# A second 2x2 scheme inside a pair of feed-forward blocks: product 4 joins product 2

## The chip, the cores and the metric

The kernel runs on one core of a Trainium2 chip. The metric is the device time of one execution in microseconds, the median of several runs; smaller is better. TensorE (PE) multiplies, with weights loaded by its own load path (PEld); VectorE (DVE), ScalarE (ACT) and GpSimd (POOL) do the element-wise work; SyncE (SP) issues nearly all transfers.

## What is computed

One layer of a decoder trunk on 1056 tokens (1024 of a prompt and 32 of samples), all in float32. The change lies in the first half of its two feed-forward networks:

```
h = LN1(alpha*x + 0.5*SwiGLU_a(x))
z = h @ w_in + b_in                     # attention and a gated MLP on z
h = LN2(alpha*h + mix @ w_out)
y = LN3(alpha*h + 0.5*SwiGLU_b(h))
def swiglu(x, w1, w3, w2):              # w1, w3: 1024 x 2816, w2: 2816 x 1024
    return (jax.nn.silu(x @ w1) * (x @ w3)) @ w2
```

## The kernel before

**Precision.** A float32 number is split in a rounded high part and the rest: ACT casts the high part (line 254), DVE subtracts it from the number (line 255). Each 128x128x264 product then takes three matmuls (`mm3`, line 243): high by high, high by low, low by high.

**Seven products for eight.** A block f is 128 columns of w1 together with the same 128 of w3. Its work is a 2x2 matrix product: the rows are w3 and w1, the inner halves are the two halves of the 1024 inputs, the columns are two neighbouring pieces of 264 tokens. There are two such column pairs, `x` = 0 and 1. The Strassen-Winograd scheme does it in seven products, numbered 1 to 7 and used in the order 1, 2, 6, 7, 5, 4, 3 or near it. One product is KH = 4 slices of 128 inputs x 2 column pairs x 3 matmuls = 24 matmuls (`product`). The combined weights are made for each block by `parts13`: two loads of 512 KB (`ab` is w3, `cd` is w1), four sums on POOL (lines 445, 446, 450, 451; on DVE for the first blocks), and six splits into tiles W. The combined inputs (`self.T`) are made once for a stage by `spread`.

**A pair of blocks.** Product 2 uses the second input half of w3 alone. For two successive blocks f and g it is again a 2x2 product: the rows are the blocks, the inner halves are halves of those 512 inputs, the columns are x = 0 and 1. `hidden_pair` therefore does the two product 2 together in seven inner products of 2 x 3 = 6 matmuls, 42 rather than 48; their weights come from `parts_two` (one load, four sums of 256 columns on POOL, three splits), their inputs from `spread_two`, once a stage. So a pair has 6 x 2 outer products of 24 and 42 inner matmuls, 330. `half` is the generator that runs one block's outer products. There are ten pairs in each of the two networks; in the first, one block is left over and runs before them in `hidden`.

**Around it.** After a pair `spill_sums` makes seven combinations of the hidden values for the w2 stage, four of them by a subtraction on DVE (line 701), splits them and stores them (lines 697, 698). It runs in the background queue `bg`; each call of `step` takes three pieces from that queue and moves the next block's `parts13` on by one piece. `ready(f)` finishes the weights of f and starts those of the block after it. `advance(two)` moves `parts_two` on.

**Buffers.** Tiles named W are weights (8 buffers); R are raw loads and Q the sums on POOL (2 each); M (6) and S (37) are working tiles. PSUM has 3 banks `mm` and 5 `ax`; outer products use mostly ax, inner ones mm.

**Order.** A list scheduler (`schedule_with_timeline_sim=True`) places each engine's instructions by its own estimate of readiness; work inside `urgent()` goes ahead of other ready work. Each engine then runs its list strictly in order.

Of the kernel before, what the change touches and what calls it, by code (L numbers as in the profile page):

```python
# [21 lines left out]
P = 128  # L22
# [62 lines left out]
class Trunk:  # L85
# [339 lines left out]
    def parts13(self, src, f, engine):  # L425
# [22 lines left out]
        part(4, cd[:, hi])  # L448
# [12 lines left out]
    def parts_two(self, w13, f):  # L461

        nc, H, q = self.nc, KH * P, KH * P // 2
        with self.tc.high_priority(offset=URGENT):
            raw = self.R([P, D]).rearrange("p (f x) -> p f x", f=2)
            dma = nc.sync.dma_start(raw, w13[f : f + 2, 1, :, H:].rearrange("f p x -> p f x"))
# [11 lines left out]
        one, four = self.S([P, 2, H], F32R), self.M([P, 2, q], F32R)  # L478
# [3 lines left out]
        h, l = self.S([P, 4, q], F32R), self.S([P, 4, q], F32R)  # L482
        self.split(h, l, s)
        self.L2 = {1: (one[:, 0, :q], one[:, 1, :q]), 2: (one[:, 0, q:], one[:, 1, q:]), 4: (four[:, 0], four[:, 1])}
        for i, p in enumerate((5, 6, 7, 3)):
            self.L2[p] = (h[:, i], l[:, i])
        yield

    def spread_two(self, y0, y1):

        nc = self.nc
        b11, b21, b12, b22 = y0[:, :2], y0[:, 2:], y1[:, :2], y1[:, 2:]
        one, two = self.T[0][2], self.T[1][2]
        rows = lambda hi, lo: [(hi[:, k], lo[:, k]) for k in range(2)]
        pick = lambda t, o: [x[:, o : o + 2] for x in t]
        T = self.T2 = {1: rows(*pick(one, 0)), 2: rows(*pick(one, 2)), 3: rows(*pick(two, 2))}

        def sub(a, b):
            t = self.M([P, 2, C])
            nc.vector.tensor_tensor(t, a, b, op=ALU.subtract)  # L500
            return t

# [7 lines left out]
        t1 = sub(b12, b11)  # L510
        yield
        t2 = sub(b22, t1)
        put(5, t1, pick(two, 0))
        yield
        t3 = sub(b22, b12)
        put(6, t2)
        yield
        t4 = sub(b21, t2)
# [66 lines left out]
    def half(self, f):  # L585
# [16 lines left out]
        go(three, 7, lambda x: copy(h[:, x, 1], three[x]), True)  # L602
        yield h
        go(one, 6, lambda x: copy(h[:, x, 0], one[x]))
        yield
        go(three, 4, lambda x: tt(h[:, x, 0], three[x], h[:, x, 0], op=ALU.add))
        yield
        go(one, 5, lambda x: tt(h[:, x, 1], one[x], h[:, x, 1], op=ALU.add))  # L608
        with self.urgent():
            for x in range(2):  # L610
                nc.scalar.activation(h[:, x], h[:, x], AF.Silu)  # L611
# [4 lines left out]
    def hidden_pair(self, f, g, w13, ready, step):  # L616

        nc = self.nc
        copy = nc.scalar.copy
        two = self.parts_two(w13, f)  # L620
        a, b = self.half(f), self.half(g)
# [1509 lines left out]
```

## Time and profile before

| what | value |
|---|---|
| median of 3 runs | 2142.72 us (2141.47 to 2144.37) |
| the profiled execution's own time | 2141.25 us |
| its span, first to last instruction | 2139.3 us, mean clock 0.994 |
| busy: PE, DVE, ACT, POOL | 98%, 74%, 44%, 17% of the span |
| DMA | 436.99 MB, mean 204 GB/s |

The pairs of the first network run from about 66 to 455 us, those of the second from about 1400 to 1860 us; the w2 stages follow them. In the rows of the profile, a group reads: line, engine, operation, output<-input by the program's names, shapes, count | busy us, mean ns of one | idle time of the engine just before, and what ended most of it. In a list by order of time the first two numbers are the start and the duration in us.

### The profile page before, as it was taken

What the parts mean: (1) busy time and instruction counts of PE and PEld (TensorE: products, weight loads), DVE (VectorE), ACT (ScalarE), POOL (GpSimd) and SP (SyncE); (2) the same over time, 40 slices, a digit from 0 to 9 for tenths busy, and PEclk for the clock granted to TensorE, in tenths of its full rate; (3) what the DMA queues carried; (4) which work ended last, traced back from release to release, by engine and by line L of the source; (5) the groups of instructions that cost most, each with busy time, mean ns of one, the idle gap of its engine ahead of it and who ended that gap; (6) DMA issues with size and microseconds to landing.
All of it is one profiled execution on the core that took longest, in us unless ns stands there. A gap on an engine that the chain in (4) does not pass through costs nothing.

```text
span 2139.3 us, 43300 instructions
## 1 busy us (share of the span) xinstructions
PE 2103.2 (98%) x17163; PEld 2069.3 (97%) x17163; DVE 1587.7 (74%) x2915; ACT 941.0 (44%) x1897; POOL 363.8 (17%) x329
## 2 busy tenths in 40 slices
PE   9999999999999999999999989999999999999997
PEld 8999999998999999999988889999999999999997
DVE  8877777767789846988767558787777777757886
ACT  5544444422124643445476543164545545522224
POOL 0234334300000022332000000000433433300000
PEclk9999999999999999999999999999999999999998
DMA  4365565599884346676756655432446545597852
GB/s 155 117 206 175 184 222 175 180 367 354 306 332 176 123 144 213 221 250 216 276 190 198 195 166 173 151 118 98 168 172 213 194 138 183 202 355 294 307 180 82
DMA packets 172954, 436.99 MB, mean 204 GB/s; under 512 B 24576, under 2 KB 58992, under 8 KB 170064
## 3 DMA queue, kind: packets, MB, share of 16 engines
q1 hardware_dynamic: 172320, 433.70, 58.0%
q8 instruction: 134, 2.20, 0.4%
q14 instruction: 68, 0.56, 0.1%
q10 hardware_dynamic: 432, 0.54, 0.1%
HBM read 314.80 MB, written 165.57 MB: 225 GB/s over the span
## 4 chain that ended last, share of the span: by engine, by line
PE 87%; DMA 7%; DVE 4%; SPq 1%; issue 1%; ACT 1%; ACTq 0%; DVEq 0%
PE ax L243 48%; PE mm L243 35%; DMA S<-sumsA 1%; DMA R<-w2pb 1%; DMA R<-w2pa 1%; DMA S<-sumsB 1%; DMA S<-hD 1%; PE ax L1428 1%; PE ax L1477 1%; DMA S<-cD 1%; PE ax L1454 1%; DVE W L255 0%; DVE S L843 0%; DVE S L255 0%; DMA cD<-S 0%
## 5 line engine op out<-in xcount | busy, mean ns | idle before, releaser
L243 PE MATMUL ax<-S,W 128*128 128x264 f32 x7392 | 989.5, 285 | 5.2 <-ACT W L254 4.9
L243 PEld LDWEIGHTS ax<-S,W 128*128 128x128 f32 x7392 | 936.9, 188 | 7.2 <-ACT W L254 5.4
L243 PE MATMUL mm<-S,W 128*128 128x264 f32 x5232 | 735.4, 287 | 14.2 <-DVE S L1807 4.8
L243 PEld LDWEIGHTS mm<-S,W 128*128 128x128 f32 x5232 | 674.7, 189 | 25.4 <-DVE S L1807 6.7
L243 PE MATMUL mm<-S,S 128*128 128x264 f32 x1944 | 284.5, 286 | 0.8 <-DVE S L1147 0.6
L243 PEld LDWEIGHTS mm<-S,S 128*128 128x128 f32 x1944 | 255.2, 188 | 2.6 <-issue 0.6
L254 ACT CAST W<-R 128x512 fp32r<-128x512 f32 (+4 forms) x214 | 137.6, 658 | 245.3 <-PE mm L243 66.2
L255 DVE TENSOR_TENSOR W<-R,W 128x512 fp32r<-128x512 f32 (+4 forms) x214 | 175.5, 824 | 67.2 <-ACT W L254 65.7
L243 PE MATMUL ax<-S,S 128*128 128x264 f32 x1488 | 218.0, 284 | 0.0
L243 PEld LDWEIGHTS ax<-S,S 128*128 128x128 f32 x1488 | 196.4, 188 | 0.2 <-issue 0.2
L255 DVE TENSOR_TENSOR W<-Q,W 128x512 fp32r<-128x512 f32 (+2 forms) x199 | 148.2, 761 | 57.5 <-ACT W L254 57.2
L254 ACT CAST W<-Q 128x512 fp32r<-128x512 f32 (+2 forms) x199 | 128.6, 678 | 81.9 <-DVE Q L392 78.4
L1042 DVE SCALAR_TENSOR_TENSOR S<-ax,S 128x264 f32<-128x264 f32 x240 | 99.4, 429 | 51.7 <-PE ax L243 51.0
L111 POOL CAST S<-ones 128x1 fp32r<-128x1 f32 x36 | 12.8, 363 | 625.7 <-PE ax L243 381.5
L611 ACT ACTIVATE S<-S 128x528 f32<-128x528 f32 x80 | 47.2, 638 | 140.9 <-DVE S L608 140.9
L255 DVE TENSOR_TENSOR S<-Q,S 128x1024 fp32r<-128x1024 f32 (+1 forms) x59 | 65.6, 1113 | 25.2 <-ACT S L254 25.2
L445 POOL TENSOR_TENSOR Q<-R 128x512 f32<-128x512 f32 x36 | 48.1, 1335 | 204.0 <-DVE W L255 74.5
L1256 ACT ACTIVATE S<-ax,cols 128x264 f32<-128x264 f32 (+5 forms) x99 | 40.4, 496 | 87.5 <-PE ax L243 83.1
L473 POOL TENSOR_TENSOR Q<-R 128x256 f32<-128x256 f32 x20 | 20.9, 1045 | 341.0 <-DVE W L255 270.3
L254 ACT CAST S<-Q 128x1024 fp32r<-128x1024 f32 (+1 forms) x59 | 56.9, 965 | 34.6 <-DVE Q L403 32.1
L651 DVE TENSOR_TENSOR M<-M,M 128x264 f32<-128x264 f32 x60 | 63.4, 1083 | 11.2 <-ACT M L657 11.2
L599 ACT COPY M<-ax 128x264 f32<-128x264 f32 x80 | 26.9, 376 | 95.1 <-issue 88.1
(246 smaller groups left out, 2305.8 us busy)
## 6 DMA issues: line engine op xcount, KB each, us to landing
ws<-st SPq DMA_DIRECT2D x144, 256.0 KB
S<-sumsA SPq DMA_DIRECT2D x63, 528.0 KB
S<-sumsB SPq DMA_DIRECT2D x63, 528.0 KB
R<-w13b SPq DMA_DIRECT2D x54, 512.0 KB
R<-w13a SPq DMA_DIRECT2D x52, 512.0 KB
M<-kv SPq DMA_DIRECT2D x96, 256.0 KB
sumsA<-M SPq DMA_DIRECT2D x90, 264.0 KB
sumsB<-M SPq DMA_DIRECT2D x90, 264.0 KB
```

The costliest lines, as they stand in the source:

```text
L243: mm = lambda a, b, s, e: nc.tensor.matmul(o, a[:, cc], b, start=s, stop=e, skip_group_check=True)
L254: a = self.nc.scalar.copy(hi, src)
L255: b = self.nc.vector.tensor_tensor(lo, src, hi.bitcast(F32), op=ALU.subtract)
L445: tt(s12[:, lo], cd[:, lo], cd[:, hi], op=ALU.add)
L599: go(one, 1, lambda x: copy(r[:, x], one[x]), True)
L611: nc.scalar.activation(h[:, x], h[:, x], AF.Silu)
L651: nc.vector.tensor_tensor(t, t, m, op=ALU.add)
L1042: nc.vector.scalar_tensor_tensor(y(x, r, e), bank[x], HALF, y(x, r, e), op0=ALU.mult, op1=ALU.add)
L1256: nc.scalar.activation(o, view(bank[x]), fn, bias=b, scale=sc)
L1428: m = nc.tensor.matmul(pS[h][:, r, :nk], q[e, i * P : (i + 1) * P], k[e, k0 : k0 + nk], start=True, stop=True)
L1454: nc.tensor.transpose(pT[r][:, h, o], s[:, r, h, o], self.ident)
L1477: nc.tensor.matmul(pv[0][e, (i % 4) * P : (i % 4 + 1) * P], V[:, i - (nb - 1) + b, e], sT[:, r, h, b * P : b * P + P], start=b == 0, stop= ...
```

## The change

Product 4 uses the second input half of w1 alone, so the two products 4 of a pair form a 2x2 product in the same way. The change treats them as product 2 was treated: `parts_two` takes a `row` (1 for w3, 0 for w1) and is called twice for a pair, `spread_two` takes the product's number n and is called for 2 (on DVE, as before) and for 4 (its eight sums and differences on POOL: the inputs are first put together again from their parts). `parts13` no longer makes the part for product 4, so it has five splits. A pair is 5 x 2 outer products and 2 x 42 inner matmuls, 324.

It also rearranges the pair: the seven inner products for w3 now run among the outer products of the first block, those for w1 among the second's. Most inner results are added by DVE straight from PSUM to the accumulators; before, ACT copied more of them out and DVE added the copies. `parts_two` of the next pair's w3 (`ahead`) is made during this pair. The weights of the inner products move from S to W tiles. `ready(g)` is called one product earlier. In `spill_sums`, three of the four subtractions go from DVE to POOL.

```diff
     def parts13(self, src, f, engine):
...
-        part(4, cd[:, hi])
...
-    def parts_two(self, w13, f):
+    def parts_two(self, w13, f, row):
...
-            dma = nc.sync.dma_start(raw, w13[f : f + 2, 1, :, H:].rearrange("f p x -> p f x"))
+            dma = nc.sync.dma_start(raw, w13[f : f + 2, row, :, H:].rearrange("f p x -> p f x"))
...
-        one, four = self.S([P, 2, H], F32R), self.M([P, 2, q], F32R)
+        one, four = self.W([P, 2, H]), self.M([P, 2, q], F32R)
...
-        h, l = self.S([P, 4, q], F32R), self.S([P, 4, q], F32R)
+        h, l = self.W([P, 4, q]), self.W([P, 4, q])
...
-    def spread_two(self, y0, y1):
+    def spread_two(self, n, engine, *raw):
...
+        def value(j, o):
+            if raw:
+                return raw[j][:, o : o + 2]
+            return make(*(x.bitcast(F32) for x in pick(self.T[j][n], o)), ALU.add)
...
     def half(self, f, r=None):
...
-        one, r = (ax(), ax()), self.M([P, 2, C])
-        go(one, 1, lambda x: copy(r[:, x], one[x]), True)
+        one = ax(), ax()
+        if r is None:
+            r = self.M([P, 2, C])
+            go(one, 1, lambda x: copy(r[:, x], one[x]), True)
+        else:
+            go(one, 1, lambda x: tt(r[:, x], r[:, x], one[x], op=ALU.add), True)
...
-        go(one, 6, lambda x: copy(h[:, x, 0], one[x]))
-        yield
-        go(three, 4, lambda x: tt(h[:, x, 0], three[x], h[:, x, 0], op=ALU.add))
+        go(one, 6, lambda x: tt(h[:, x, 0], one[x], h[:, x, 1], op=ALU.add))
...
+    def inner(self, row, p, bank, act, first=False):
+        n = 2 if row else 4
+        while p not in self.T2.get(n, ()):
+            self.step(self.bg, 1)
+        for k in range(2):
+            self.mm3(bank, self.L2[row].pop(p) if k else self.L2[row][p], k * P, *self.T2[n][p][k], first and k == 0, k == 1)
+        with self.urgent():
+            act(bank)
+
+    def hidden_pair(self, f, g, ready, step, two, ahead):
...
+        r = next(a)
+        step(f)
+        x, y = bank(), bank()
+        do(1, 1, x, add(r[:, 0]), True)
+        do(1, 2, y, add(r[:, 0]), True)
+        h = next(a)
+        step(f)
+        self.advance(two)
+        do(1, 6, x, copy(s[:, 0]))
+        y = bank()
+        do(1, 7, y, copy(s[:, 1]), True)
+        next(a)
...
+        do(1, 5, x, add(s[:, 1]))
+        do(1, 4, y, add(s[:, 0]))
+        next(a)
...
+        next(b)
...
+        ready(g)
+        do(1, 3, x, add(r[:, 1]))
+        next(a)
...
+        i = next(b)
+        step(g)
+        self.advance(ahead)
+        x, y = bank(), bank()
+        do(0, 1, x, add(h[:, 0, 0]), True)
+        do(0, 2, y, add(h[:, 0, 0]), True)
...
     def spill_sums(self, i, a, b):
...
-        sub = lambda t, u, v: nc.vector.tensor_tensor(t, u, v, op=ALU.subtract)
+        sub = lambda t, u, v, e=nc.gpsimd: e.tensor_tensor(t, u, v, op=ALU.subtract)
...
     def ffn(self, w13, w2p, w2, i, mode, resid):
...
+        twos = [lambda y=(self.Y[0][1], self.Y[2][1]): self.spread_two(2, nc.vector, *y)]
+        twos.append(lambda: self.spread_two(4, nc.gpsimd))
...
+            for _ in ahead:
+                pass
+            ready(f)
+            ahead = two(queue[0], 1) if queue else None
+            self.hidden_pair(f, g, ready, step, two(f, 0), ahead)
```

What the scheduler makes of it at the passage from one pair to the next. Line numbers are each kernel's own. POOL before, the four sums of one block's weights (into Q) and the four of `parts_two`:

```order
L445 TENSOR_TENSOR Q_2231<-R_2194 128x512
L446 TENSOR_TENSOR Q_2231<-Q_2231,R_2193 128x512
L450 TENSOR_TENSOR Q_2280<-R_2193,R_2194 128x512
L451 TENSOR_TENSOR Q_2280<-R_2193,Q_2231 128x512
L473 TENSOR_TENSOR Q_2370<-R_2289 128x256
L475 TENSOR_TENSOR Q_2370<-R_2289 128x256
```

POOL now, the same place (445, 446, 449 and 450 are the weights' sums, 719 the spill's subtractions):

```order
L445 TENSOR_TENSOR Q_2296<-R_2258 128x512
L719 TENSOR_TENSOR S_1818<-S_2062,S_1818 128x2x264
L719 TENSOR_TENSOR M_2300<-S_2062,M_2299 128x528
L449 TENSOR_TENSOR Q_2359<-R_2257,R_2258 128x512
L446 TENSOR_TENSOR Q_2296<-Q_2296,R_2257 128x512
L719 TENSOR_TENSOR M_2362<-S_2062,M_2300 128x528
L450 TENSOR_TENSOR Q_2359<-R_2257,Q_2296 128x512
```

Three subtractions stand between the four sums, and each is behind a sum that needs a loaded R tile. DVE before, from the last products of a pair (line 678) on; 701 are the spill's subtractions, 255 the splits:

```order
L678 TENSOR_TENSOR S_1743<-S_1743,M_1694 128x2x264
L255 TENSOR_TENSOR W_2147<-Q_2032,W_2147 128x512
L613 TENSOR_TENSOR S_2002<-S_2002,ax_1910 128x264
L613 TENSOR_TENSOR S_2002<-S_2002,ax_1911 128x264
L701 TENSOR_TENSOR M_2234<-S_1743 128x528
L701 TENSOR_TENSOR M_2235<-S_2002,M_2234 128x528
L701 TENSOR_TENSOR S_1743<-S_2002,S_1743 128x2x264
L255 TENSOR_TENSOR W_2228<-R_2193,W_2228 128x512
L255 TENSOR_TENSOR S_1743<-S_1743,M_2237 128x2x264
L255 TENSOR_TENSOR M_2234<-M_2234,M_2243 128x528
```

DVE now, there (638 are inner results added from a bank mm, 615 an outer one from ax):

```order
L696 TENSOR_TENSOR S_1818<-S_1818,M_1752 128x2x264
L719 TENSOR_TENSOR M_2299<-S_1818 128x528
L255 TENSOR_TENSOR W_2254<-Q_2188,W_2253 128x1024
L638 TENSOR_TENSOR M_2266<-M_2266,mm_2314 128x264
L255 TENSOR_TENSOR W_2293<-R_2257,W_2293 128x512
L255 TENSOR_TENSOR S_1818<-S_1818,M_2304 128x2x264
L638 TENSOR_TENSOR M_2266<-M_2266,mm_2315 128x264
L615 TENSOR_TENSOR S_2332<-ax_2264,S_2332 128x264
L255 TENSOR_TENSOR M_2299<-M_2299,M_2309 128x528
L615 TENSOR_TENSOR S_2332<-ax_2265,S_2332 128x264
L255 TENSOR_TENSOR S_1818<-S_1818,M_2364 128x2x264
```

The evictions of mm and ax now stand between splits with both inputs in SBUF; before, only the splits and subtractions stood here.

More of the change, by code (lines that the diff above doesn't have):

```diff
@@ L609, in half @@
         with self.urgent():
-            for x in range(2):
-                nc.scalar.activation(h[:, x], h[:, x], AF.Silu)
+            nc.scalar.activation(h[:, :, 1], h[:, :, 1], AF.Silu)
         yield
@@ L623, in hidden_pair @@
+    def hidden_pair(self, f, g, ready, step, two, ahead):
+        nc = self.nc
+        bank = lambda: self.mm_tile()[:, :C]
+        copy = lambda t: lambda b: nc.scalar.copy(t, b)
+        add = lambda t: lambda b: nc.vector.tensor_tensor(t, t, b, op=ALU.add)
+        do = self.inner
+        s = self.M([P, 2, C])
+        a, b = self.half(f), self.half(g, s)
+        r = next(a)
         step(f)
-        h.append(next(a))
+        x, y = bank(), bank()
+        do(1, 1, x, add(r[:, 0]), True)
+        do(1, 2, y, add(r[:, 0]), True)
+        h = next(a)
@@ L636, in hidden_pair @@
         ready(g)
+        do(1, 3, x, add(r[:, 1]))
+        next(a)
+        step(g)
+        self.advance(two)
         del self.L[f]
-        while len(self.T2) < 7:
-            self.step(self.bg, 1)
-        def inner(p, bank, act, first=False):
-            hi, lo = self.L2[p]
-            for k in range(2):
-                self.mm3(bank, (hi, lo), k * P, *self.T2[p][k], first and k == 0, k == 1)
-            with self.urgent():
-                act()
-        def add(t, *more):
-            def act():
-                for m in more:
-                    nc.vector.tensor_tensor(t, t, m, op=ALU.add)
-            return act
@@ L655, in hidden_pair @@
-        one, two = self.mm_tile()[:, :C], self.mm_tile()[:, :C]
-        tu, v = self.M([P, 2, C]), self.M([P, C])
-        inner(1, one, lambda: copy(tu[:, 0], one), True)
-        inner(2, two, add(r[0][:, 0], tu[:, 0], two), True)
-        step(g)
-        h.append(next(b))
-        step(g)
-        inner(6, one, lambda: copy(tu[:, 1], one))
-        three = self.ax_tile()[:, :C]
-        inner(7, three, lambda: copy(v, three), True)
+        i = next(b)
+        step(g)
+        self.advance(ahead)
@@ L665, in hidden_pair @@
+        x, y = bank(), bank()
+        do(0, 1, x, add(h[:, 0, 0]), True)
+        do(0, 2, y, add(h[:, 0, 0]), True)
         next(b)
         step(g)
-        inner(5, one, add(r[1][:, 1], v, one))
+        self.advance(ahead)
+        do(0, 6, x, add(i[:, 0, 0]))
+        y = bank()
+        do(0, 7, y, add(i[:, 1, 0]), True)
         next(b)
         step(g)
-        next(b)
-        step(g)
-        inner(4, three, add(r[1][:, 0], tu[:, 1], three))
-        inner(3, one, add(r[0][:, 1], one))
@@ L674, in hidden_pair @@
-        step(g)
-        next(b)
-        with self.urgent():
-            for x, y in zip(h, r):
-                nc.vector.tensor_tensor(x[:, :, 0], x[:, :, 0], y, op=ALU.mult)
-        self.L2 = None
-        step(g)
+        self.advance(ahead)
+        do(0, 5, x, add(i[:, 1, 0]))
+        do(0, 4, y, add(i[:, 0, 0]))
+        step(g)
+        self.advance(ahead)
+        next(b)
+        do(0, 3, x, add(h[:, 1, 0]))
+        with self.urgent():
+            for t, u in ((i, s), (h, r)):
+                nc.scalar.activation(t[:, :, 0], t[:, :, 0], AF.Silu)
+                nc.vector.tensor_tensor(t[:, :, 0], t[:, :, 0], u, op=ALU.mult)
```

84 lines of the change are left out of this document (42 added, 42 removed).

## The prediction

> **What bounds the kernel now.** I read the page's totals first, then the waits of the matmul engine, then the stage that the change touches in stretches as long as one pair of blocks, then its groups by shape, and last the order of time where VectorE (DVE) and GpSimd (POOL) meet.
>
> ```profile
> span 2139.3 us, 43300 instructions
> PE 2103.2 (98%) x17163; PEld 2069.3 (97%) x17163; DVE 1587.7 (74%) x2915; ACT 941.0 (44%) x1897; POOL 363.8 (17%) x329
> PE 87%; DMA 7%; DVE 4%; SPq 1%; issue 1%; ACT 1%; ACTq 0%; DVEq 0%
> ```
>
> TensorE is busy for 98% of the span and makes 87% of the chain that ended last. The list of what it waited for is short:
>
> ```profile
> engine line waited for: us in total, times, longest us
> PE ax L243 <- ACT W L254: 4.9, 2, 3.6
> PE mm L243 <- DVE S L1807: 4.8, 6, 2.1
> PE mm L243 <- DVE S L1147: 3.6, 4, 1.7
> ```
>
> Asked for 60 to 455 us and for 1400 to 1860 us alone, the two stretches with the pairs, the list has a heading and no row: there TensorE never waits. Stretches of 40 us (columns: us, then PE, weight load, DVE, ACT, POOL busy with their counts, granted clock, DMA share, GB/s):
>
> ```profile
> 112.00:152.00 40.00, 40.00 (x330) 40.00 (x330) 29.34 (x47) 19.44 (x42) 14.32 (x13) 1.00 0.52 173
> 152.00:192.00 40.00, 40.00 (x331) 40.00 (x329) 29.61 (x47) 19.45 (x41) 14.65 (x12) 1.00 0.56 193
> 192.00:232.00 40.00, 40.00 (x331) 40.00 (x330) 29.79 (x47) 18.67 (x40) 14.72 (x12) 1.00 0.56 185
> 66.00:106.00 40.00, 40.00 (x331) 40.00 (x331) 33.51 (x52) 21.80 (x49) 14.70 (x12) 1.00 0.37 113
> 1398.00:1438.00 40.00, 40.00 (x331) 39.94 (x330) 34.35 (x52) 26.95 (x51) 1.67 (x6) 1.00 0.30 107
> ```
>
> A pair has 12 products of 24 matmuls and 7 inner ones of 6, 330 in all, and 330 to 331 matmuls pass in 40.00 us at clock 1.00: 0.121 us each, 40.0 us a pair, set by TensorE's own rate. DVE has 10.4 us of 40 free, ACT 20, POOL 25.
>
> **The change, part by part.** *Matmuls.* The fourth products of two blocks, 2 x 24, become 7 x 6 = 42. There are 10 pairs in each of the two stages, so 20 x 6 = 120 matmuls go, 120 x 0.121 = **14.5 us**, all on the path. A pair is then 324 matmuls, 39.2 us. This is paid in full only if the other engines still keep ahead. Their prices come from these rows (112 to 232 us, three pairs, so a third of each count is one pair):
>
> ```profile
> L255 DVE TENSOR_TENSOR W<-Q,W 128x512 fp32r<-128x512 f32 x24 | 16.0, 686 | 7.9 <-ACT W L254 7.9
> L651 DVE TENSOR_TENSOR M<-M,M 128x264 f32<-128x264 f32 x9 | 10.2, 1155 | 2.0 <-ACT M L657 2.0
> L608 DVE TENSOR_TENSOR S<-ax,S 128x264 f32<-128x264 f32 x12 | 4.7, 426 | 2.7 <-PE ax L243 2.7
> L678 DVE TENSOR_TENSOR S<-S,M 128x528 f32<-128x528 f32 x6 | 4.0, 702 | 0.0
> L651 DVE TENSOR_TENSOR M<-M,mm 128x264 f32<-128x264 f32 x9 | 3.9, 430 | 1.9 <-PE mm L243 1.4
> L255 DVE TENSOR_TENSOR S<-Q,S 128x1024 fp32r<-128x1024 f32 x3 | 3.7, 1226 | 1.8 <-ACT S L254 1.8
> L255 DVE TENSOR_TENSOR M<-R,M 128x256 fp32r<-128x256 f32 x3 | 1.3, 419 | 0.0
> L254 ACT CAST W<-Q 128x512 fp32r<-128x512 f32 x24 | 13.9, 618 | 0.0
> L254 ACT CAST S<-Q 128x1024 fp32r<-128x1024 f32 x3 | 3.2, 1052 | 0.0
> L254 ACT CAST M<-R 128x256 fp32r<-128x256 f32 x3 | 1.2, 403 | 0.0
> L604 ACT COPY S<-ax 128x264 f32<-128x264 f32 x12 | 4.4, 380 | 9.9 <-PE ax L243 9.9
> ```
>
> *DVE.* Undisturbed, an operation with both inputs in SBUF takes 0.69 us at 512 columns, 0.70 at 528, 1.23 at 1024, 0.42 at 256 and some 0.43 at 264; one that reads a PSUM bank takes 0.43. Before, a pair has 12 splits of parts13 (8.2), one parts_two (0.69 + 0.42 + 1.23 = 2.3), 7 splits of the spill (4.9), 4 subtractions (2.8), 2 last products (1.4), 3 sums M<-M,M (1.3): 21.0 us with two SBUF inputs, and 16 evictions (6.9 us). After: 10 splits (6.9), two parts_two (4.7), 4.9, one subtraction (0.7), 1.4: 18.5 us, and 26 evictions (11.2 us), since most of those that ACT copied are now added by DVE. DVE's own work goes from 27.9 to 29.7 us a pair, +1.8. *ACT* casts 0.62 + 0.40 + 1.05 - 2 x 0.62 = +0.8 us and loses 7 copies of 0.38: -1.8 us, never near a limit.
>
> *POOL.* Four more subtractions of 256 columns for the second parts_two, and three of 528 that DVE did. It is also here that two engines get in each other's way:
>
> ```profile
> L446 POOL TENSOR_TENSOR Q<-Q,R 128x512 f32<-128x512 f32 x6 | 9.1, 1517 | 0.2
> L476 POOL TENSOR_TENSOR Q<-R,Q 128x256 f32<-128x256 f32 x3 | 2.2, 742 | 0.2
> 280.47 1.29 POOL L445 TENSOR_TENSOR Q<-R 128x512 f32<-128x512 f32 x1 [7.29 <-DMA R<-w13a]
> 281.74 1.28 POOL L450 TENSOR_TENSOR Q<-R,R 128x512 f32<-128x512 f32 x1
> 282.98 1.73 POOL L446 TENSOR_TENSOR Q<-Q,R 128x512 f32<-128x512 f32 x1
> 284.79 1.36 POOL L451 TENSOR_TENSOR Q<-R,Q 128x512 f32<-128x512 f32 x1
> 281.75 1.81 DVE L255 TENSOR_TENSOR W<-R,W 128x512 fp32r<-128x512 f32 x1 [1.59 <-ACT W L254]
> 283.49 2.96 DVE L651 TENSOR_TENSOR M<-M,M 128x264 f32<-128x264 f32 x2
> ```
>
> Alone, POOL takes 1.29 us for 512 columns and 0.74 for 256, so about 1.33 for 528 (estimate). The DVE split that started with a POOL operation took 1.81 us in place of 0.69, the 264-column sums 1.5 each in place of 0.43; each ended shortly after the POOL operation beside it. POOL's next then took 1.73: the two take turns. Operations that read PSUM (426 and 430 ns) show none of it. From 283.02 to 284.71 a POOL operation and a 0.69 us DVE one passed in 1.69 us, so a turn of DVE costs POOL 0.40, not 0.69; from 284.71 to 286.15 a 0.43 us one cost 0.15.
>
> POOL per pair: 8 x 1.29 + 4 x 0.74 = 13.3 us now, 8 x 1.29 + 8 x 0.74 + 3 x 1.33 = 20.2 after. What must take turns is 21.0 + 13.3 = 34.3 of 40.0 us now, and 18.5 + 20.2 = 38.7 of 39.2 after; with 0.28 saved at each of 19 turns (0.69 - 0.40, 0.43 - 0.15), 33.4. That is tight, and this is the whole risk. The Trainium skill, page "SBUF — State Buffer", section "Who interferes with whom", states that a VectorE instruction with two SBUF inputs contends with a GpSimd instruction that reads SBUF, and that the pair of ports is held for the full instruction. By that rule alone the sum of turns would be the 38.7 us, almost no room; the rows agree on who blocks whom (1155 against 430 ns) but not that nothing overlaps (0.40, not 0.69).
>
> *The stretch that decides* is the one of the order above, where a pair's spill subtractions stand in POOL's queue between the four operations of the next weights: seven POOL operations in a row, while DVE has five or six two-input operations with evictions between them and behind them. A held-up DVE operation holds the evictions queued behind it, and TensorE needs a bank again one product later at the earliest: 24 x 0.121 = 2.9 us, less 0.43 for the eviction leaves 2.5 us. Seven turns at 1.69 are 11.8 us, about 100 matmuls; before, four of them are 6.8. In the rows above DVE lost 1.1 us three times within 5 us, and TensorE did not wait. So the bounds for the stall of one steady pair are 0 and one more POOL operation, 1.3 us. I take 0.2, nearer the row that shows three such losses covered, because the chain of turns is nearly twice as long: 18 pairs x 0.2 = **+3.6 us** (0 to 23).
>
> *First pair of each stage.* The inner products now begin after the first outer one, so the operands spread for product 2 are due some four products earlier, and those for product 4 are new: 4 splits (2.8 us of DVE) and 8 POOL operations (10.6 us). DVE is busiest just there, 33.5 and 34.4 of 40 us, and still nothing waits. Bounds: 0 and the longest wait that TensorE shows anywhere, 3.6 us; I take 1.5 for each stage: **+3.0 us**.
>
> *Loads.* One read of 512 KB more in each pair, so the two raw buffers turn over six times in 39.2 us, not five: 13.1 us for each load.
>
> ```profile
> 275.47 0.33 SPq L432 DMA_DIRECT2D R<-w13a  x1
> ```
>
> This load was issued at 275.47 and released POOL at 280.47, 5.0 us; four POOL operations in turns use it up in 6.8: 11.8 of 13.1, which fits by a little. The DMA share of 0.52 to 0.56 leaves room on the wires. In SP's queue the new load stands behind the wait for POOL that frees its buffer, and the spill's stores behind it; they are late by what POOL is late, and their cover is the following block. Eight weight buffers serve 16 allocations a pair in place of 12: 19.6 us each, against a few us to fill and one or two products to use. The state copies that go with each load are issued sooner, the same number in all: nothing. Weights begun one product sooner: nothing by itself, since no wait of TensorE names them; it is what gives the second block its slack.
>
> **Sum.** -14.5 + 3.6 + 3.0 = -7.9 us on the profiled execution's 2141.25 us (span 2139.3 and 1.95 around it): 2133.4. The median of the runs is 1.5 above the profiled one, so 2134.8; I say 2135.
>
> **Rivals.** *The turns saturate (slower).* If DVE's evictions fall mostly outside POOL's operations they add to the 33.4 us. At a share x of the 11.2 us the pair takes 33.4 + 11.2x: above 39.2 from x = 0.52, and slower than now by 0.2% (40.2 us) from x = 0.61. At two thirds it is 40.9, +0.9 x 20 = 18: 2161 us. For it: the sum of turns, and that both queues are in order. Against it: POOL works in bursts and evictions run freely beside it. By the skill's rule, without the 0.28 at each turn, this would decide already from x = 0.13. Chance 0.15.
>
> *Gain eaten (no change).* The same hold-up costs 0.6 us a pair, half a POOL operation: -14.5 + 10.8 + 3 = -0.7, so 2142. For it: 11.8 of 13.1 us on the raw buffers leaves little to absorb. Chance 0.21.
>
> *All hidden.* Nothing stalls: 2128. For it: the empty list of waits. This is the lower end of the forecast case.
>
> **From these to the numbers.** The forecast, most of the gain kept (2127 to 2138), has 0.64. The runs here spread by 0.14%, so 0.2% (4.3 us) is about what a measurement can tell from no change. Faster 0.64; within, 0.20; slower, 0.16. The range starts at the whole gain with a us of spread, 2127, and reaches into the saturated case, 2155; beyond it I leave some 0.1 on the slow side. The likeliest case alone is 2127 to 2138.
>
> **What would show it.** 120 matmuls fewer; pair-long stretches with 330 matmuls still in 40.0 us and PE full; POOL near 22 us there (20.2, and the tenth of it that POOL loses now: 14.6 for 13.3) and DVE 32 to 35 of 40; ACT near 18. If the stall term is right, the list of PE's waits now has rows on DVE's evictions (L615, L617, L638) of a few tenths, once a pair; if the rival is, those rows make 20 us or more, DVE is over 37 of 40 us and its splits L255 average well over 0.9 us. Rows naming ACT's cast into W or the DMA into R would mean that the buffers, which I costed at nothing, are the limit. It would be wrong in the good direction if no row appears at all.

## The result, and the profile after

The changed kernel takes 2226.3 us (2223.0 to 2227.4), the kernel before beside it 2142.1: a ratio of 1.039 (95% interval 1.038 to 1.040). It is 84 us slower, where 2135 was forecast. The page of the changed kernel (totals, then the chain that ended last by engine):

```profile
span 2222.2 us, 43479 instructions
PE 2120.6 (95%) x17043; PEld 2065.3 (93%) x17043; DVE 1657.2 (75%) x3029; ACT 911.4 (41%) x1785; POOL 567.5 (26%) x479
PE 11%; DMA 6%; DVE 6%; POOL 4%; issue 3%; ACT 2%; SPq 0%; DVEq 0%; POOLq 0%; ACTq 0%
```

TensorE makes 120 matmuls fewer, as it should. Its 11% of the chain can't be set against the 87% of before: the row adds up to about a third, because this chain could be followed back only to 1527 us. In the second network's pairs the two can be compared, from 1540 to 1850 us. Before, the chain there is TensorE alone (first row below, by line); now TensorE has 5.4 us of it, under 2%, so that what ends last no longer runs through TensorE. The rows under it are stretches of 40 us in the pairs (columns as before):

```profile
by line: PE ax L243 75.9%; PE mm L243 24.1%
```

```profile
152.00:192.00 40.00, 37.10 (x294) 35.88 (x293) 28.66 (x49) 15.54 (x30) 22.46 (x19) 1.00 0.53 182
192.00:232.00 40.00, 37.26 (x298) 36.28 (x297) 28.29 (x47) 15.94 (x33) 21.26 (x17) 1.00 0.60 213
232.00:272.00 40.00, 37.00 (x292) 35.75 (x292) 28.91 (x48) 14.22 (x29) 22.23 (x18) 1.00 0.58 202
```

292 to 298 matmuls pass where 330 did: a pair of 324 takes 324/294 x 40 = 44.1 us instead of 39.2. And no engine is full: DVE idles for 11 us of 40, POOL for 18, ACT for 25, the clock is 1.00. TensorE's own waits, over the whole run, are spread over many rows. These are the five longest; apart from one wait of 7.1 us and one of 5.3, both at the start of a w2 stage, no wait in them is over 2.2 us:

```profile
PE ax L243 <- DVE S L615: 17.4, 18, 1.6
PE ax L243 <- ACT W L254: 12.4, 2, 7.1
PE mm L243 <- ACT M L637: 11.9, 15, 2.2
PE mm L243 <- DVE M L638: 9.9, 15, 1.5
PE mm L243 <- DVE W L255: 8.3, 22, 1.3
```

The list doesn't say why the evictions (L615, L638), the copy into the M buffer (L637) and the splits (L255) are late. The chain of waits does. This is its order of time in the second network's pairs (start, us, what: engine, tile written, line), one pair long, from one load of w1/w3 into R to the same load of the next pair:

```profile
1732.43 3.54 DMA R<-w13b
...
1736.11 1.28 POOL Q L445
1737.39 1.24 POOL Q L449
1738.63 1.26 POOL Q L446
...
1739.92 0.63 ACT W L254
...
1743.70 1.30 DVE W L255 x2
...
1745.13 1.06 POOL Q L472
1746.19 0.89 POOL Q L474
1747.08 1.17 POOL Q L473
...
1748.32 1.20 POOL Q L475
...
1749.54 3.64 DMA R<-w13b
...
1754.60 0.64 POOL S L719
...
1756.36 1.32 POOL M L719
...
1757.70 1.78 DVE M L255
...
1760.36 5.44 DMA sumsB<-M
...
1765.88 0.64 ACT M L254
...
1767.72 1.00 PE mm L243 x6
1768.72 1.71 PE ax L243 x14
...
1773.37 1.22 DVE W L255
...
1777.09 3.48 DMA R<-w13b
```

The reader is to see a closed round. A load lands in R; POOL sums it for the outer weights; ACT and DVE split the sums into W; that frees Q, so that POOL can make the sums of the pair weights (L472 to L475); that frees R for the next load; behind that load's sums POOL reaches the spill's subtractions (L719); DVE splits their result into M; the store of it must land before the M buffer can take the next cast; DVE's queue goes on from there to the splits that free R for the next pair's load. From load to load it is 44.7 us, about a pair's length by the count of matmuls, with 2.7 us of TensorE. The round ahead of it takes 44.0 without one piece of TensorE in it: 11.9 us of transfers, 9.6 POOL, 9.1 DVE, 4.2 ACT, 8.5 "issue" (time for which the chain names no wait; where POOL's subtractions follow, a sum of POOL is under way in it). Each link waits for the one before; no share of busy time can show that. The chain of this run doesn't reach the first network's pairs, which lose nearly as much (below); in q_from_s, whose run is as long, it does, and there loads and stores are 21% of it and TensorE 12% from 112 to 432 us.

By stage, from the start times of four rows that both traces have (first w2 eviction of each network, last product of the second network's block 0, the end):

| stretch | before, us | after, us | difference | matmuls before, after | lost |
|---|---|---|---|---|---|
| start to the first w2 eviction, first network | 455.9 | 485.0 | +29.1 | 3655, 3561 | 40.5 |
| from there to the last product of block 0, second network | 1028.8 | 1043.0 | +14.2 | 8288, 8340 | 7.9 |
| from there to the first w2 eviction, second network | 397.7 | 427.2 | +29.5 | 3264, 3143 | 44.1 |
| from there to the end | 256.9 | 267.0 | +10.1 | 1963, 2006 | 4.9 |

The first w2 evictions stand some 35 and 43 matmuls earlier in TensorE's work now, block 0's last product 18 later, so the times alone mislead. The last column takes the matmuls out, at 0.121 us each (29.1 + 94 x 0.121 = 40.5). By that the two stretches with the pairs lose 84.6 us, 4.2 a pair, and the rest 12.8; less the 14.5 us saved that is 82.9, the difference of the spans. Most of the 12.8 comes as the w2 stages begin: in the first one, from 470 to 520 us, the list of TensorE's waits has

```profile
PE ax L243 <- ACT W L254: 7.1, 1, 7.1
```

and before, from 440 to 520 us, that row has 3.6 us; for both stages together it has 12.4 us now and 4.9 before. Behind these waits the granted clock falls to a half (stretches of 5 us of the changed kernel, columns as above):

```profile
495.00:500.00 5.00, 0.00 (x0) 0.00 (x0) 1.14 (x3) 0.60 (x2) 0.00 (x0) 0.78 1.05 406
500.00:505.00 5.00, 3.07 (x14) 3.08 (x15) 3.59 (x7) 1.57 (x2) 0.00 (x0) 0.50 0.87 308
505.00:510.00 5.00, 5.00 (x31) 5.00 (x31) 4.28 (x10) 2.21 (x4) 0.00 (x0) 0.69 0.98 343
```

At the starts of the two w2 stages TensorE works for 10.5 us at clock 0.50, before for 3.0: by an estimate from these, some 4 us more lost.

### The profile page after: what moved, and what is told of

Read it like the earlier page. It is cut to its first block, busy times and chain, and to the rows that moved or that the text cites. A ratio compares the mean times of both kernels' runs of the same rounds, so it can differ in the third digit from the quotient of the medians.

```text
span 2222.2 us, 43479 instructions
## 1 busy us (share of the span) xinstructions
PE 2120.6 (95%) x17043; PEld 2065.3 (93%) x17043; DVE 1657.2 (75%) x3029; ACT 911.4 (41%) x1785; POOL 567.5 (26%) x479
## 5 line engine op out<-in xcount | busy, mean ns | idle before, releaser
L243 PE MATMUL ax<-S,W 128*128 128x264 f32 x6912 | 926.1, 286 | 35.2 <-DVE S L615 17.4
L243 PEld LDWEIGHTS ax<-S,W 128*128 128x128 f32 x6912 | 876.2, 189 | 44.1 <-DVE S L615 21.2
L243 PE MATMUL mm<-S,W 128*128 128x264 f32 x6192 | 856.3, 288 | 48.3 <-ACT M L637 11.9
L243 PEld LDWEIGHTS mm<-S,W 128*128 128x128 f32 x6192 | 789.7, 189 | 74.1 <-ACT M L637 15.1
L255 DVE TENSOR_TENSOR W<-Q,W 128x512 fp32r<-128x512 f32 (+2 forms) x239 | 227.1, 969 | 124.9 <-ACT W L254 124.5
L254 ACT CAST W<-Q 128x512 fp32r<-128x512 f32 (+2 forms) x239 | 168.9, 738 | 268.4 <-POOL Q L446 133.3
L254 ACT CAST W<-R 128x512 fp32r<-128x512 f32 (+4 forms) x214 | 137.2, 655 | 225.3 <-DMA R<-w2pa 62.3
L255 DVE TENSOR_TENSOR W<-R,W 128x512 fp32r<-128x512 f32 (+4 forms) x214 | 169.2, 794 | 43.5 <-ACT W L254 40.5
L243 PE MATMUL mm<-S,S 128*128 128x264 f32 x1344 | 197.3, 288 | 1.1 <-DVE S L1180 1.1
L243 PEld LDWEIGHTS mm<-S,S 128*128 128x128 f32 x1344 | 177.9, 191 | 2.7 <-DVE S L1180 1.1
L111 POOL CAST S<-ones 128x1 fp32r<-128x1 f32 x36 | 13.1, 373 | 619.8 <-DMA R<-w2pa 154.6
L255 DVE TENSOR_TENSOR M<-M,M 128x528 fp32r<-128x528 f32 x70 | 77.4, 1105 | 66.3 <-POOL M L719 38.5
L472 POOL TENSOR_TENSOR Q<-R 128x256 f32<-128x256 f32 x40 | 37.1, 928 | 281.8 <-DVE W L255 241.7
L254 ACT CAST M<-S 128x528 fp32r<-128x528 f32 x72 | 45.4, 631 | 117.7 <-DVE M L255 117.7
L255 DVE TENSOR_TENSOR S<-S,M 128x528 fp32r<-128x528 f32 x72 | 72.9, 1012 | 7.9 <-ACT M L254 7.9
L254 ACT CAST M<-M 128x528 fp32r<-128x528 f32 x70 | 44.0, 632 | 60.1 <-DMA sumsB<-M 22.2
```

The lines of the kernel that those rows point to most:

```text
L111: self.nc.gpsimd.tensor_copy(t[:, 0, :1] if len(shape) == 3 else t[:, :1], self.ones[:, :1])
L243: mm = lambda a, b, s, e: nc.tensor.matmul(o, a[:, cc], b, start=s, stop=e, skip_group_check=True)
L254: a = self.nc.scalar.copy(hi, src)
L255: b = self.nc.vector.tensor_tensor(lo, src, hi.bitcast(F32), op=ALU.subtract)
L472: tt(s[:, 0], a21, a22, op=ALU.add)
```

## The experiments

Times below are medians; the ratio is to the kernel before, timed beside each, with its 95% interval. "Saved" is against the changed kernel's 2226.3.

| run | built on | us | ratio | saved |
|---|---|---|---|---|
| spill_on_dve | after | 2246.3 | 1.049 (1.047 to 1.050) | -20 |
| q_from_s | after | 2223.6 | 1.038 (1.037 to 1.040) | 3 |
| s_from_s | after | 2229.2 | 1.041 (1.039 to 1.042) | -3 |
| raw_from_s | after | 2237.3 | 1.044 (1.042 to 1.047) | -11 |
| raw_s_spill_dve | after | 2210.4 | 1.032 (1.030 to 1.033) | 16 |
| subs_left_out | after | 2147.9 | 1.003 (1.002 to 1.004) | 78 |
| subs_tiny | after | 2187.3 | 1.021 (1.019 to 1.023) | 39 |
| t4_from_s | after | 2199.3 | 1.026 (1.025 to 1.028) | 27 |
| gap_one | after | 2248.6 | 1.050 (1.048 to 1.051) | -22 |
| gap_three | after | 2195.7 | 1.025 (1.023 to 1.026) | 31 |
| gap_four | after | 2177.5 | 1.017 (1.016 to 1.019) | 49 |
| gap3_t4_from_s | after | 2193.1 | 1.024 (1.022 to 1.027) | 33 |
| spill_order_before | after | 2198.7 | 1.026 (1.025 to 1.028) | 28 |
| before_pool_subs | before | 2138.9 | 0.998 (0.997 to 1.000) | |
| before_gap_one | before | 2141.5 | 1.000 (0.999 to 1.001) | |
| before_weights_in_w | before | 2134.5 | 0.997 (0.996 to 0.998) | |
| before_more_load | before | 2172.9 | 1.015 (1.014 to 1.017) | |
| before_all_three | before | 2180.0 | 1.018 (1.016 to 1.020) | |

**First theories: turns, two buffers, DVE's work.** Theory A was the prediction's own rival (POOL and DVE in each other's way), B a loop through the two buffers each of Q and R, C simply too much work on DVE.

```diff
 # spill_on_dve
-        sub = lambda t, u, v, e=nc.gpsimd: e.tensor_tensor(t, u, v, op=ALU.subtract)
+        sub = lambda t, u, v, e=nc.vector: e.tensor_tensor(t, u, v, op=ALU.subtract)
 # q_from_s (parts_two)
-        s = self.Q([P, D]).rearrange("p (i x) -> p i x", i=4)
+        s = self.S([P, D]).rearrange("p (i x) -> p i x", i=4)
```

> The changed kernel with the three spill subtractions back on DVE, nothing else. Theory A (turns at the passage: the POOL subtractions between the weights' sums hold up DVE's splits and with them the evictions that TensorE needs): the stalls at the passage from pair to pair (evictions L615, copies L637, evictions L638) go for the most part; they are 2.7 us of the 4.4 us that a steady pair loses, so 18 x 2.7 = 48 us less, about 2178. Theory B (the loop through the two buffers each of Q and R sets the length of a pair, 44.1 us): POOL's chain is shorter by 4.7 us only at one of its two places, the loop is closed by the buffers, not by the turns; under 15 us gained, 2212 or more. Theory C (DVE has simply too much work): DVE gets 2 us a pair more, so slower, over 2226.

2246.3: A had asked for a large gain and is out; the run is 20 us slower, which B and C both allowed. From one load of w1/w3 to the same load of the next pair (1611.09 to 1654.57 us of its chain), 43.5 us, 20.6 are on DVE, 11.4 are transfers and none TensorE, where the changed kernel's round (above) has 9.1 of 44.0 on DVE: the links changed engine and the path still closes without TensorE.

> The changed kernel with the sums of parts_two in a tile of S, so that they no longer wait for one of the two Q buffers (that is, for the last split that reads the weights' sums). Theory B: POOL's idle 6.5 and 2.6 us ahead of L472 go, the next load starts sooner, a pair falls from 44.1 towards 40 us: over 50 us gained, 2176 or less. Theory A: only the two stalls outside the passage can go (row-0 evictions L638 and the first split of the next pair, 0.73 + 0.32 us a pair): at most 20 us, 2206 to 2226.

2223.6: the Q buffers alone are not it.

```diff
 # s_from_s (hidden_pair)
-        s = self.M([P, 2, C])
+        s = self.S([P, 2, C])
 # raw_from_s (parts_two); raw_s_spill_dve is this and spill_on_dve together
-            raw = self.R([P, D]).rearrange("p (f x) -> p f x", f=2)
+            raw = self.S([P, D]).rearrange("p (f x) -> p f x", f=2)
```

> The changed kernel with the accumulator of the inner results (written by the copies L637) in a tile of S, not M, so that those copies no longer wait for a store of the spill to land. A and B alike would give the 0.9 us a pair that TensorE waits on L637 if it is a cause of its own: 16 us, 2210. If it only hides behind the other stalls (the next eviction is late by as much), under 5 us: 2221 to 2226.

2229.2: one long-held M tile fewer brought nothing; the copy L637 then waits for a slot that a store frees, for 32 us in all from 112 to 432 us (in the changed kernel for an M tile, 13 us).

> The changed kernel with the raw load of parts_two in a tile of S, so that the two R buffers serve the loads of parts13 alone (four a pair, not six). Theory B, in its present form: a pair's 44 us are one loop, twice round: load into R 3.7 us, POOL's sums, ACT's cast and DVE's split of part 6, the eviction and SiLU queued behind it, the casts of parts 7, 5, 3, parts_two's sums on POOL, its split of raw on DVE, and only then the buffer is free for the next load. Taking raw out of R takes the two loads (7.4 us) and the splits of raw out of the loop: 44.1 - 7.4 = 36.7 us, under the 39.2 that TensorE needs. So a pair falls to 39.2 to 40.5 us and the kernel to 2130 to 2160. Theory C (DVE's work, with the turns against POOL, is what is too long): nothing of DVE's or POOL's work changes, so 2215 or more.

2237.3, 11 us slower with the raw load taken out of R: R alone is not it either, in the form that B had. Why it is slower is not shown: its mean granted clock is 0.982 (the changed kernel: 0.990), 0.97 for 1.00 from 112 to 432 us, and over the whole run that difference can cost up to 18 us (estimate, 0.008 x 2237).

> As raw_from_s, and the three spill subtractions back on DVE. B: they added 20 us when the loop had no slack, because they stand ahead of the weights' splits in DVE's queue; with slack they are hidden, and this is within 5 us of raw_from_s. C: 15 to 25 us over raw_from_s, as over the changed kernel.

2210.4. Two edits that each cost time gain 16 us together (27 against raw_from_s, whose lower clock may be a part of it). Neither B (within 5 us of raw_from_s) nor C (15 to 25 us over it) has that; it was the first sign that several links stand in one round.

**The three subtractions alone.**

```diff
 # before_pool_subs, on the kernel before
-        sub = lambda t, u, v: nc.vector.tensor_tensor(t, u, v, op=ALU.subtract)
+        sub = lambda t, u, v, e=nc.gpsimd: e.tensor_tensor(t, u, v, op=ALU.subtract)
-        sub(t1, x12, x11)
+        sub(t1, x12, x11, nc.vector)
 # subs_left_out, on the changed kernel
-        sub(x12, x22, x12)
-        sub(t2, x22, t1)
+        t2 = x21
-        t4 = self.M([P, 2, C])
-        sub(t4, x21, t2)
-        yield from out(4, t4)
+        yield from out(4, t1)
```

> The kernel before with the three spill subtractions on POOL: this one part of the change alone. Theory A: three more turns in POOL's queue at the passage, but no evictions are queued behind DVE's splits there in this kernel, so little: 0 to 10 us slower. Theory B: the loop has time to spare in this kernel (POOL idle 25 of 40 us), no change within 4 us. Theory C: DVE loses 2 us of work a pair, no change or a little faster.

> The changed kernel with the three spill subtractions of POOL left out altogether (what is stored for those products is then not the reference's sum; the splits and stores stay). Theory A: the turns at the passage fall from 7 to 4, 2 to 2.7 us a pair, 36 to 48 us less than 2226. B: POOL's part of the loop is shorter by the 3 subtractions at one of its two places only, 1.6 x 2 (the third stands behind the sum that part 6 waits for): about 3 us a pair, 55 us less. C: DVE loses no work, only waits of up to 3 us: 20 us less. So this tells A and B from C, and with the run that put them on DVE says what a subtraction costs in either queue.

On the kernel before they are harmless (2138.9); left out of the changed kernel they are worth 78 us, more than A (36 to 48), B (55) or C (20) expected. Its pairs then run near TensorE's rate:

```profile
192.00:232.00 40.00, 39.92 (x327) 39.57 (x325) 32.85 (x53) 18.84 (x37) 21.56 (x18) 1.00 0.65 220
```

Leaving them out also frees the M tiles t2 and t4, so the chain of waits above was read next, and theory D was made of it: the round as a whole is the limit. Its rival M is that the six M buffers alone are.

**Cutting the round at one link each.**

```diff
 # subs_tiny: 4 of 264 columns; two splits read another tile
+        few = lambda *x: sub(*(t[:, :, :4] for t in x))
-        sub(x12, x22, x12)
-        sub(t2, x22, t1)
+        few(x12, x22, x12)
+        few(t2, x22, t1)
-        sub(t4, x21, t2)
+        few(t4, x21, t2)
-        yield from out(6, t2)
+        yield from out(6, t2, x22)
-        yield from out(4, t4)
+        yield from out(4, t4, x21)
 # t4_from_s
-        t4 = self.M([P, 2, C])
+        t4 = self.S([P, 2, C])
 # gap_one, gap_three, gap_four
-GAP = 2
+GAP = 1, 3 or 4
```

> The three subtractions of the spill on POOL work on 4 of 264 columns in each half, and the splits behind two of them read another tile of the right size, so the sums' values are not the reference's. Tiles, buffers, stores, queue order and the splits stay as in the changed kernel; only the subtractions' duration goes. The chain of waits of the changed kernel is a closed round through the pairs that TensorE is not part of: load of w1/w3 into R (3.5 us), POOL's sums, splits into W, POOL's sums of the pair weights, the next load (3.7), two of POOL's spill subtractions (0.6 and 1.3 on the chain, with 1.1 us of start ahead of each), DVE's split into M, the store's landing that frees M (4.7 to 5.4), ACT's cast into M, DVE's splits, the next load: 44 us in all. Theory D (the round as a whole is the limit): without some 4 us of it the round falls under TensorE's 39.2 us, 2140 to 2160. Rival M (the six M buffers alone, which t2 and t4 hold until their stores land): the tiles are still there, so 2200 or more.

> The sixth operand of the spill, t4, comes from the slots S instead of the M buffers. Rival M: one of the ten M tiles that a spill takes is gone, the landing of a store (4.7 to 5.4 us) leaves the round once, pair 44 to about 40: 2150 to 2190. Theory D: the landing on the chain is that of an earlier store, and the subtractions stay: 2205 to 2230. If DVE's and POOL's time alone were it: 2226, no change.

> The spill waits for three steps instead of two between its seven operands (GAP 3), so that each store has about half as long again to land before the next cast asks for an M buffer. Theory D and rival M: the landing wait leaves the round, but the spill runs later into the next pair and holds the slots of the hidden tiles longer: 2190 to 2220. If the engines' time were it: 2226, no change.

> The spill waits for one step between its operands (GAP 1): the M buffers are asked for sooner after each store. Theory D and rival M: every landing is waited for in full, 2235 to 2270. If the engines' time were it: 2226, no change.

2187.3, 2199.3, 2195.7 and 2248.6. The subtractions' bare time is worth 39 us with every tile in place (two splits also no longer read what POOL wrote), a buffer 27, later stores 31, and tighter stores cost 22. Both kinds of link carry the delay, so M alone is out. But D was not met in size: subs_tiny fell between the two theories, 27 us above D's 2160 and 13 below M's 2200, and so did t4_from_s (M 2190 or less, D 2205 or more). In subs_tiny the store's landing still stands on the chain (14.6% of it from 1640 to 1700 us, where TensorE has 35%), which fits. In gap_one two long waits for the M buffer come at the ends of the two stages, 11.7 us from 470 to 520 us and 10.7 from 1950 to 2000; in its steady pairs TensorE waits for an eviction, once a pair. Its mean clock is 0.980 in the trace, so a part of the 22 us may be the clock:

```profile
PE ax L243 <- DVE S L617: 39.8, 17, 4.0
PE mm L243 <- ACT M L637: 27.5, 7, 11.7
```

> The changed kernel with three steps between the spill's operands and t4 in the slots S, both of the runs that recovered 31 and 27 us. Theory D (a round of waits in which the landing of the stores is only one link): the landing is now off the round, the loads and POOL's queue remain near TensorE's 39.2 us; no more than 10 us below gap_three, 2180 to 2196. Rival M (the six M buffers are all of it): the two add up, 2150 to 2175.

> Four steps between the spill's operands: 35 of the pair's 42 background steps. Theory D: the landing was already off the round with three, and the spill's last operands now hold the hidden tiles' slots longer and come later into the w2 stage: 2185 to 2210. Rival M: once more faster than gap_three, 2165 to 2190.

2193.1: two cuts at the same link, worth 31 and 27 alone, bring 33 together, as D expected, and TensorE's longest row of waits is now another link, the splits into W:

```profile
PE mm L243 <- DVE W L255: 28.6, 19, 3.1
```

gap_four, 2177.5, went against D and with M: a still later store gains another 18 us. So either the landing was not yet off the round with three steps, or later stores help in another way; the chain of that run doesn't reach its steady pairs.

**The order of the spill.** The change also put all three POOL subtractions ahead of the spill's first store; before, each stands just ahead of the operand that it makes.

```diff
 # spill_order_before
         sub(t1, x12, x11, nc.vector)
-        sub(x12, x22, x12)
-        sub(t2, x22, t1)
         yield from out(1, x11)
+        sub(t2, x22, t1)
         yield from out(5, t1)
+        sub(x12, x22, x12)
+        yield from out(7, x12)
         t4 = self.M([P, 2, C])
         sub(t4, x21, t2)
-        yield from out(7, x12)
```

> The changed kernel with the spill written in the order of the kernel before: each subtraction stands just ahead of the operand that it makes, still on POOL, instead of three ahead of the first store. Theory D: POOL's queue has one subtraction at a time between the weights' sums, so that a late load holds up one of them and not three, but M and R turn over as often: 2195 to 2220. Rival O (the order is all of it, since the same operations on POOL in the old order are harmless in the kernel before): 2150 to 2180. If neither order nor place matters: 2226.

2198.7, 28 us saved, inside D's range and far from O's: the order is one more link, not all of it.

**The parts one at a time in the kernel before, then together.**

```diff
 # before_weights_in_w (parts_two)
-        one, four = self.S([P, 2, H], F32R), self.M([P, 2, q], F32R)
+        one, four = self.W([P, 2, H]), self.M([P, 2, q], F32R)
-        h, l = self.S([P, 4, q], F32R), self.S([P, 4, q], F32R)
+        h, l = self.W([P, 4, q]), self.W([P, 4, q])
 # before_more_load: a generator advanced three times in a pair's second half
+            raw = self.R([P, D]).rearrange("p (f x) -> p f x", f=2)
+            nc.sync.dma_start(raw, w13[f : f + 2, 0, :, H:].rearrange("f p x -> p f x"))
+        s = self.Q([P, D]).rearrange("p (i x) -> p i x", i=4)
+        tt(s[:, 0], a21, a22, op=ALU.add)
+        tt(s[:, 1], s[:, 0], a11, op=ALU.subtract)
+        tt(s[:, 2], a11, a21, op=ALU.subtract)
+        tt(s[:, 3], a12, s[:, 1], op=ALU.subtract)
 # before_gap_one: GAP = 1
```

> The kernel before with one step between the spill's operands instead of two. Theory D: its round has several us of slack and takes the full wait for the stores' landing, 2140 to 2150. Rival M: the M buffers are as tight there as in the changed kernel, where the same edit cost 22 us: 2155 or more.

> The kernel before with the pair weights (three tiles a pair) in the eight W buffers instead of slots, 15 allocations a pair for 12. Theory D: the pair weights' splits now wait for W to come free, POOL's Q buffers and the raw buffer behind them, but the round keeps slack with one set of them: 2140 to 2155. Rival W (the W buffers are what closes the round): 2165 or more, with PE waits that name the split into W.

> The kernel before with one more raw load of 512 KB into R and four more sums of 256 columns on POOL in each pair, in the second half, whose result nobody reads; everything else as before. If the sixth turnover of the two R buffers closes the round by itself: 2165 or more. Theory D: the kernel before still has its slots for the pair weights and DVE does the spill's subtractions, so that the round stays below 40 us: 2140 to 2150.

The tighter M buffers cost nothing (2141.5, against 22 us in the changed kernel). The pair weights in W even gain 0.3% (2134.5). Its steady stretches pass 331 matmuls in 40 us as before; the gain shows where the first w2 stage begins (593 matmuls from 445 to 520 us for 563, and the wait for L254 there is 0.8 us for 3.6). Why was not followed up. The sixth load costs 31 us, against D's number. But its steady pairs are full, and it is at the w2 stages that it waits (a stretch in the pairs; then TensorE's waits from 440 to 520 us):

```profile
192.00:232.00 40.00, 40.00 (x329) 39.88 (x328) 32.69 (x48) 19.25 (x41) 18.40 (x16) 1.00 0.60 207
```

```profile
PE ax L243 <- ACT W L254: 11.0, 2, 10.7
```

By the stretches of the table (the matmuls in them are those of before, within five), the pairs lose 3.0 and 3.9 us and the two stretches with the w2 stages 13.9 and 9.9: there the last pair's extra load stands ahead of the first w2 weights. So the steady round had room for it; the end of a stage had not.

> The kernel before with the three parts together that were tried there alone: the spill's subtractions on POOL (in the old order), the sixth load with its four sums on POOL (whose result nobody reads; not in a stage's last pair, so that it does not stand ahead of the w2 weights), and the pair weights in W. Its order of products, its evictions and its 330 matmuls a pair stay. Theory D (the links add up to a round that is too long): PE waits in the steady pairs, 2160 or more. Rival P (the new order of products and evictions, in which each pair's two sets of pair weights hold W through a half pair and DVE makes nearly all evictions, is needed for the round): the steady pairs stay at TensorE's rate and the run within 10 us of the kernel before, 2133 to 2150.

2180.0: together, and without the extra load in a stage's last pair, they close the round in the old kernel, old order of products and 330 matmuls and all. Rival P is out. Counted as in the table, with the matmuls taken out, the pairs lose 23.3 and 21.7 us and the stretches behind them nothing (-4.0 and -1.7). A part of that is the clock, 0.98 on average from 112 to 432 us; the stretch shown is at 1.00. The stretch, then the chain in the second network, from an eviction's end to the same eviction of the next pair:

```profile
232.00:272.00 40.00, 38.28 (x312) 37.93 (x311) 31.60 (x43) 19.18 (x40) 22.10 (x19) 1.00 0.59 195
```

```profile
1647.39 3.32 PE ax L243 x25
...
1664.98 0.63 ACT W L254
...
1665.63 0.70 DVE W L255
...
1669.61 1.07 POOL Q L503
...
1670.70 3.30 DMA R<-w13b
...
1676.88 1.77 POOL M L722
1678.65 1.28 POOL S L722
1679.93 1.74 POOL Q L446
...
1682.34 1.61 DVE W L255
...
1689.33 0.35 DVE S L625
...
1689.72 3.32 PE ax L243 x25
```

42.3 us a round (330/312 x 40 gives the same), and all three parts stand in it: a W buffer that TensorE frees at 1664.98, the extra sums (L503) whose end frees R for the load, the subtractions on POOL (L722) ahead of the weights' sum L446. TensorE is in it for 17.6 us and waits once a pair. It is not link for link the round of the changed kernel: no store's landing stands in it. No two of the three parts were tried without the third.

## Why the prediction was wrong, point by point

- **The matmuls, -14.5 us: right in number.** 17043 for 17163. No run shows them paid in full: with the subtractions left out the profiled execution is still 1.0 us longer than the one before. From 66 to 112 us, about the first pair, it passes 341 matmuls for 380, 4.7 us late; in the steady pairs it nearly keeps pace (326 to 329 in 40 us).
- **The steady pair's stall, 0.2 us (bounds 0 and 1.3): the step that failed.** A steady pair takes 44.1 us instead of 39.2, a stall of 4.9. With the first pairs the two terms were 6.6 us; measured, some 85 for the 20 pairs. The bound was taken from what a held-up DVE operation costs the eviction behind it, so from one stretch of the order. The delay is a round through four queues (SP, POOL, ACT, DVE) and four kinds of buffers (R, Q, W, M), whose length no single stretch bounds.
- **Loads at nothing, "11.8 of 13.1 us fits by a little"; W buffers at nothing; POOL's subtractions inside the sum of turns: each right alone, wrong together.** The kernel before absorbs each in its steady pairs; the three together cost it 45 us there, about half of what the changed kernel loses. I asked of each whether it fits the pair, not whether they stand behind one another.
- **The M buffers: not in the working at all.** I named R and W and left out the pool of six, whose tiles wait for a store that takes 4.5 to 5.4 us to land. t4_from_s, gap_three and gap_four show that it is one of the links, worth 27 to 49 us.
- **The spill's order: not costed.** I counted its subtractions and not where they stand; spill_order_before puts 28 us on that.
- **The w2 stages: not in the sum.** The stretches behind the pairs lose 12.8 us, most of it in the waits at the start of the w2 stages and the half clock behind them. That a load too many near a stage's end costs time there is seen in the kernel before: before_more_load loses 13.9 and 9.9 us, before_all_three, without that load in a stage's last pair but different in two other parts as well, none. Which load or buffer it is in the changed kernel was not tried.
- **The first pairs, 3.0 us for both: too small.** TensorE's waits from 30 to 115 us come to 3.2 us in the first network alone, and from 66 to 112 us it passes 348 matmuls for 380, 3.9 us. It is not what decides.
- **The durations: POOL's too short.** POOL is at 21 to 22.5 us of 40, the figure of the forecast, but of a pair of 44.1 us that is some 24, for 22 expected. The 528-column subtraction, estimated at 1.33 undisturbed, takes 1.59 on average, the 256-column sums up to 1.10 for 0.74; DVE's splits of 512 columns go from 0.69 to 0.89 (the rows, from 112 to 232 us, are below). DVE (28 to 29 of 40) and ACT (14 to 16) came out below the forecast 32 to 35 and 18, in the main because the pair is longer.
- **Rival "turns saturate":** the direction was right and the mechanism wrong. Of its signs the rows on evictions came, 35 us in all (L615, L617, L638); but it asked for DVE over 37 of 40 us, where 28 to 29 is busy, and moving the subtractions to DVE makes it slower. The Trainium skill, page "SBUF — State Buffer", section "Who interferes with whom", says who blocks whom, and the longer durations here agree; but the sum of turns (38.7 of 39.2 us by its rule) is not what the pair waited for. Turns do lengthen links of the round: on the chain shown POOL's four 256-column sums (L472 to L475) take 4.3 us for 4 x 0.74, and DVE's 528-column split 1.78 for 0.70, together 2.4 us of the 44.7.

```profile
L719 POOL TENSOR_TENSOR M<-S,M 128x528 f32<-128x528 f32 x5 | 8.0, 1594 | 0.0
L474 POOL TENSOR_TENSOR Q<-R 128x256 f32<-128x256 f32 x6 | 6.6, 1099 | 0.0
L255 DVE TENSOR_TENSOR W<-Q,W 128x512 fp32r<-128x512 f32 x24 | 20.7, 894 | 18.1 <-ACT W L254 18.1
```

- **Rivals "gain eaten" and "all hidden":** both took the stall for a fraction of one POOL operation, and fell with that bound.
- **What would show it:** the announced rows on evictions (L615, L617, L638) and on ACT's cast into W came, which let the list of waits speak for three theories at once. Only the chain told them apart.

What stays open: how the 85 us of the pairs divide over the links, since cuts at different links don't add up (39, 31, 28 and 27 us alone, 78 for the subtractions with their tiles, 33 for two at the same link). No kernel tried here with the new products beats the kernel before; before_weights_in_w, without them, beats both.

## What to carry to other kernels

Before a change adds turns to several small buffer pools, follow one buffer round: what must end for it to come free, which in-order queue that stands in, and what that queue waits for, until the path comes back to its start; the round's length, landings of stores included, has to stay below the period of the work, whatever the engines' busy shares say (here 44.0 against 39.2 us). When all engines are idle part of the time and the list of waits is spread over many short rows, read the chain in order of time and look for the same row one period later; add up its shares first, since a chain can end long before the start of the run. When two runs are compared by stage, count the matmuls in each stage beside its time: a marker can move in the order. And cost a change where a stage ends as well: the next stage's first weights stand in the same queues and buffers.

## What the runs showed of the hardware

Two edits that each lengthened the run shortened it together (raw_from_s +11 us, spill_on_dve +20, both -16). That fits links of one round, but raw_from_s also ran at a lower clock, and the two were not separated. A long wait of TensorE cost more than its own length: the changed kernel's run has six stretches with a granted clock of 0.50 behind its start, of 3.4 to 13.1 us each, and in the 4.3 us ahead of each TensorE had been busy for 1.3 to 2.5 us only. And transfers cost there by their latency, not by their share of the wires: on the changed kernel's chain through the pairs a 512 KB load took 3.4 to 4.3 us and a 264 KB store mostly 4.6 to 5.4 us until its buffer was released, with the DMA share between 0.44 and 0.62 in the stretches. I had thought of stores as work that nobody waits for.
